# A running log-sum-exp on one core: the first-row test moves from small loads to GpSimd, and the last store is made whole

## The chip, the cores and the metric

The kernel runs on one NeuronCore of a Trainium2 chip. The core has five engines, each with its own in-order queue of instructions: TensorE (PE in the profile, PEld for its weight loads), VectorE (DVE), ScalarE (ACT), GpSimd (POOL) and SyncE (SP). They meet through semaphores. SBUF is the on-chip memory of 128 partitions, PSUM the memory that matmuls write. Transfers between HBM and SBUF run on 16 DMA engines that all the queues share; a transfer is cut into packets, and here each of the 16 engines gets the same number of them. The metric is the device time of one launch in microseconds (us). The kernel before takes 1264.43 us, the median of three runs from 1264.23 to 1265.02.

## The reference

The input `x` is float32 of shape (4, 4096, 4128): four batches, 4096 steps, 4128 columns. The output is the running log-sum-exp along the steps, for each batch and column by itself:

```python
out[:, 0, :] = x[:, 0, :].copy()
for t in range(1, S):
    mx = np.maximum(out[:, t - 1, :], x[:, t, :])
    out[:, t, :] = mx + np.log(np.exp(out[:, t - 1, :] - mx) + np.exp(x[:, t, :] - mx))
```

With values of moderate size this is log(cumsum(exp(x))). That is 270.5 MB read and 270.5 MB written.

## The kernel before

`_fast` computes log(cumsum(exp(x))) directly and also computes a flag that says whether that was safe. If it wasn't, `_general` computes everything again in the reference's slow form. With the inputs here the flag is good and `_general` is branched over, so it is code that lies in the program and doesn't run.

**Tiling.** A batch has 4096 rows. A step of the kernel (`Step`) takes 128 partitions times r rows, with r = 3: partition p holds rows 3p, 3p+1 and 3p+2 of the block, all 4128 columns, so a partition's share of a load is one run of 49,536 bytes. 4096 rows make ten steps of r = 3 and one of r = 2, eleven steps a batch and 44 in all. In the first batch the step of r = 2 comes first, in the others last. The first steps of the four batches are steps 0, 11, 22 and 33. A step's tile `xt` has four buffers. It is worked on in place, in four chunks of columns (`Chunk`): three of 1024 and a rest of 1056.

**Work of a step and chunk.** ScalarE takes Exp of the whole chunk (L114). VectorE adds the rows inside a partition (`sums`, L118: one instruction for r = 2, two for r = 3, each with two operands in SBUF). TensorE multiplies the last row by a triangle of ones (`excl`), which gives every partition the sum of the partitions before it (`head`, L125; for the rest `head_rest`, L133 and L135). VectorE adds this from PSUM to all rows (`add`, L149; `add_rest`, L142). TensorE passes the total of the last partition on to the next step (`pass_on`, L158), for the rest VectorE copies it (`keep`, L154). ScalarE takes Ln (L170). Then the whole tile is stored.

**Order.** The order on every engine is written out by hand in lists (`ORDER`, `DORDER`, `PORDER`) and recorded as such (`manual_schedule`). ScalarE's order in a step is: Exp of chunks 0 and 1, Ln of chunks 2 and 3 of the step before, Exp of chunks 2 and 3, Ln of chunks 0 and 1 (`e0 e1 p2 p3 e2 e3 l0 l1`). So store k can be issued only after the second pair of Ln in step k+1. VectorE's order is `s0 s1 a0 s2 a1 s3 a2 r` and then the carry copy. In the last step ScalarE ends with Ln of chunks 2 and 3.

**SP's queue** issues every transfer: four loads at the start, the loads of first rows (below), then store k, the load of step k+3 (which waits until store k-1 has landed and its buffer is free), store k+1, and so on. DMA engines take transfers in the order of issue.

**The flag.** At a batch's end VectorE sums the totals (`total`, L165) into columns of `part`. To see a too small first value as well, `load_first` (L198) loads the four first rows of `x` a second time, as four transfers of 16 KB onto 32 partitions (`first`), and `small` (L193) in step 22 takes exp(-x) of them with its sum into one more column of `part`. After the last step `part` is reduced, one matmul sums it over the partitions (L295), and the flag is whether the sum is at most 2^40 (L296). All five engines read the flag (L351) and branch (L352).

**The last store** (`SPLIT`) is cut in two by columns: columns 0 to 2047 are stored when Ln of chunks 0 and 1 is done, the rest when the other two are.

Of the kernel before, what the change touches and what calls it, by code (L numbers as in the profile page):

```python
# [7 lines left out]
FP32 = mybir.dt.float32  # L8
INT32 = mybir.dt.int32
ACT = mybir.ActivationFunctionType  # L10
AX = mybir.AxisListType
ALU = mybir.AluOpType
P = 128
R = 3
CH = 1024
# [4 lines left out]
LAST = ["e0", "e1", "p2", "p3", "e2", "e3", "l0", "l1", "l2", "l3"]  # L20
DORDER = ["s0", "s1", "a0", "s2", "a1", "s3", "a2", "r"]
PORDER = ["h0", "h1", "p0", "h2", "p1", "r0", "r1", "p2", "r2"]
SPLIT = True
HI = 96
LIMIT = float(2 ** 40)
STEPS = 15


def _constants(nc, pool):
# [22 lines left out]
def _fast(ctx, tc, x, out, flag):  # L52


    nc = tc.nc
    B, S, D = x.shape
# [8 lines left out]
    cpool = ctx.enter_context(tc.tile_pool(name="cpool", bufs=1))  # L65
# [1 line left out]
    prest = ctx.enter_context(tc.tile_pool(name="prest", bufs=2, space=bass.MemoryType.PSUM))  # L67

    carry = cpool.tile([P, rest], FP32, name="carry")
    q = 8  # L70
    first = cpool.tile([B * q, D // q], FP32, name="first")
    part = cpool.tile([P, 4 * B + 1], FP32, name="part")
    every = cpool.tile([P, 1], FP32, name="every")
    nc.vector.memset(carry, 0.0)  # L74
    nc.vector.memset(part, 0.0)
# [22 lines left out]
    class Chunk:  # L98
# [13 lines left out]
        def exp(self):  # L112
            rows = self.rows(0, self.t.r)
            nc.scalar.activation(rows, rows, ACT.Exp)  # L114

        def sums(self):
            for j in range(1, self.t.r):
                nc.vector.tensor_tensor(  # L118
                    out=self.row(j), in0=self.row(j - 1), in1=self.row(j), op=ALU.add)
# [48 lines left out]
        def ln(self):  # L168
            rows = self.rows(0, self.t.r)
            nc.scalar.activation(rows, rows, ACT.Ln)  # L170

    steps = []
    for b in range(B):
        n = S // P
# [3 lines left out]
        row = 0  # L178
# [4 lines left out]

    chunks = [Chunk(s, c) for s in steps for c in range(4)]
    T = len(steps)
    done = set()
    act, dve, pe, sync = [], [], [], []

    def put(queue, name, work, *needs):
        queue.append((name, work, needs))  # L190

    def small():
        nc.scalar.activation(  # L193
            first, first, ACT.Exp, scale=-1.0, accum_out=part[:first.shape[0], 4 * B:4 * B + 1])

    def load_first():
        for b in range(B):
            nc.sync.dma_start(  # L198
                out=first[b * q:(b + 1) * q, :], in_=x[b, 0, :].rearrange("(q f) -> q f", q=q))

    for k, t in enumerate(steps):
        C = chunks[4 * k:4 * k + 4]
        prev = chunks[4 * k - 4:4 * k] if k else []
        W = len(subs)

        def exp(c):
            put(act, ("exp", k, c), C[c].exp, ("load", k))

        def ln(kk, c):
            put(act, ("ln", kk, c), chunks[4 * kk + c].ln, ("keep" if c == 3 else "pass", kk, c))  # L210

        order = ORDER if 0 < k < T - 1 else (FIRST if k == 0 else LAST)
        for o in order:
            if o[0] == "e":
                exp(int(o[1]))
            elif o[0] == "l":
                ln(k, int(o[1]))
            elif k:
                ln(k - 1, int(o[1]))
        if k == T // 2:  # L220
            put(act, ("small",), small, ("first",))

        def sums(c):
            put(dve, ("sums", k, c), C[c].sums, ("exp", k, c))

        def add(c):
            put(dve, ("add", k, c), C[c].add, ("head", k, c))

        for o in DORDER:
            if o[0] == "s":  # L230
                sums(int(o[1]))
            elif o[0] == "a":
                add(int(o[1]))
            else:
                for i in range(W):
                    put(dve, ("rest", k, i), lambda i=i, C=C: C[3].add_rest(i), ("headr", k, i))
        put(dve, ("keep", k, 3), C[3].keep)
        if t.last and k < T - 1:
            for c in range(4):
                put(dve, ("total", k, c), C[c].total, ("keep" if c == 3 else "pass", k, c))  # L240

        def head(c):
            put(pe, ("head", k, c), C[c].head, ("sums", k, c), ("total", k - 1, c) if k and steps[k - 1].last else ("sums", k, c))

        def headr(i):
            put(pe, ("headr", k, i), lambda C=C: C[3].head_rest(i), ("sums", k, 3),
                ("keep", k - 1, 3) if k else ("sums", k, 3), ("rest", k, i - 2) if i >= 2 else ("sums", k, 3))

        def onward(c):
            put(pe, ("pass", k, c), C[c].pass_on, ("add", k, c))  # L250

        for o in PORDER:
            if o[0] == "h":
                head(int(o[1]))
            elif o[0] == "p":
                onward(int(o[1]))
            else:
                headr(int(o[1]))

        if k < BUFS:  # L260
            put(sync, ("load", k), t.load)
    put(sync, ("first",), load_first)
    for c in range(4):
        if any(o == f"p{c}" for o in LAST) and not any(o == f"l{c}" for o in LAST):
            put(act, ("ln", T - 1, c), chunks[-4 + c].ln, ("keep" if c == 3 else "pass", T - 1, c))
    for k, t in enumerate(steps):
        if k < T - 1:
            put(sync, ("store", k), t.store, *[("ln", k, c) for c in range(4)])
            if k + BUFS - 1 < T and k:
                put(sync, ("load", k + BUFS - 1), steps[k + BUFS - 1].load, ("store", k - 1))  # L270
        elif SPLIT:
            put(sync, ("half",), lambda: steps[-1].store(0, 2 * CH), ("ln", k, 0), ("ln", k, 1))
            put(sync, ("store", k), lambda: steps[-1].store(2 * CH), ("ln", k, 2), ("ln", k, 3))
        else:
            put(sync, ("store", k), t.store, *[("ln", k, c) for c in range(4)])
    queues = [sync, act, dve, pe]
    at = [0] * 4
    while any(at[i] < len(queues[i]) for i in range(4)):
        moved = False
        for i in range(4):  # L280
            while at[i] < len(queues[i]):
                name, work, needs = queues[i][at[i]]
                if not all(d in done for d in needs):
                    break
                work()
                done.add(name)
                at[i] += 1
                moved = True
        assert moved, [queues[i][at[i]][::2] for i in range(4) if at[i] < len(queues[i])]

    for c in chunks[-4:]:
        c.total()
# [1 line left out]
    q = prest.tile([P, MM], FP32, name="q")  # L294
# [4 lines left out]
def _general(ctx, tc, x, out):  # L299

    nc = tc.nc
    B, S, D = x.shape
    q = P // B
    f = D // q
    assert P == B * q and D == q * f and (S - 1) % STEPS == 0
    one = ctx.enter_context(tc.tile_pool(name="one", bufs=1))
    state = one.tile([P, f], FP32, name="state")
    xs = one.tile([P, STEPS, f], FP32, name="xs")
    os = one.tile([P, STEPS, f], FP32, name="os")
    mx = one.tile([P, f], FP32, name="mx")  # L310
    two = one.tile([P, 2, f], FP32, name="two")

    def flat(t, b, first, n):
        return t[b, bass.ds(first, n), :].rearrange("t (q f) -> q t f", q=q)

    for b in range(B):
        nc.gpsimd.dma_start(out=state[b * q:(b + 1) * q, :].unsqueeze(1), in_=flat(x, b, 0, 1))
    for b in range(B):
        nc.gpsimd.dma_start(out=flat(out, b, 0, 1), in_=state[b * q:(b + 1) * q, :].unsqueeze(1))
    with tc.For_i(1, S, STEPS) as i:  # L320
        for b in range(B):
            nc.gpsimd.dma_start(out=xs[b * q:(b + 1) * q], in_=flat(x, b, i, STEPS))
        for j in range(STEPS):
            own = state if j == 0 else os[:, j - 1, :]
            nc.vector.tensor_tensor(out=mx, in0=own, in1=xs[:, j, :], op=ALU.max)
            nc.vector.tensor_tensor(out=two[:, 0, :], in0=own, in1=mx, op=ALU.subtract)
            nc.vector.tensor_tensor(out=two[:, 1, :], in0=xs[:, j, :], in1=mx, op=ALU.subtract)
            nc.scalar.activation(two, two, ACT.Exp)
            nc.vector.tensor_tensor(
                out=two[:, 0, :], in0=two[:, 0, :], in1=two[:, 1, :], op=ALU.add)  # L330
            nc.scalar.activation(two[:, 0, :], two[:, 0, :], ACT.Ln)
            nc.vector.tensor_tensor(out=os[:, j, :], in0=mx, in1=two[:, 0, :], op=ALU.add)
        nc.vector.tensor_copy(state, os[:, STEPS - 1, :])
        for b in range(B):
            nc.gpsimd.dma_start(out=flat(out, b, i, STEPS), in_=os[b * q:(b + 1) * q])


@with_exitstack
# [46 lines left out]
```

## Time and profile before

| What | Value |
|---|---|
| Median of three runs | 1264.43 us (1264.23 to 1265.02) |
| The profiled execution | 1264.14 us, its span 1262.7 us |
| Bytes over the span | 541.47 MB, mean 429 GB/s |
| VectorE, ScalarE, TensorE, GpSimd busy | 82%, 73%, 60%, 0% |
| A load of r = 3 from issue to landing | 43.8 us (40 of them) |
| A store of r = 3 from issue to landing | 33.1 us (40 of them) |
| The loads of first rows | 4 of 16.1 KB |
| The two parts of the last store | 2048 and 2080 KB |
| Last Ln begins; its pair takes | 1243.76 us; 3.76 us |
| The flag's comparison (L296) | at 1250.38 us |

The profile shows one execution from its first to its last instruction (the span). The time of an execution is 1.4 us longer than its span. For each engine the profile has busy time, groups of instructions by line, and what ended the idle time in front of them. The chain of waits follows the work that ended last back to the start. The windows give each engine's busy time in a stretch, the share of time that the 16 DMA engines worked, and the rate at which they moved bytes. The timeline has the instructions of one engine in order: start, duration, line, operation, output and input; the SP queue's rows are the issues of transfers. The trace also holds every DMA packet and every landing, so one can see when each of the 16 engines ended its part of a transfer.

### The profile page before, as it was taken

The numbers are of one execution on the slowest core, as the hardware profiler recorded it, in microseconds if no ns is written. First come the engines' busy times: TensorE is split into PE (matmuls) and PEld (weight loads), VectorE is DVE, ScalarE is ACT, GpSimd is POOL, SyncE is SP. The second block draws the span as 40 slices with busy tenths as digits, with TensorE's granted clock in tenths as the row PEclk, the third lists the DMA queues.
The fourth block names the chain that finished last, engine by engine and source line by source line (L and its number), as shares of the span: only waits on it lengthen the run. The fifth ranks groups of instructions, "written<-read, shape, count | busy, mean of one in ns | idle before, by whom it ended". The sixth has DMA issues, their size and how long they took to land.

```text
span 1262.7 us, 4846 instructions
## 1 busy us (share of the span) xinstructions
PE 761.7 (60%) x1562; PEld 307.1 (24%) x1562; DVE 1031.7 (82%) x664; ACT 926.7 (73%) x355; POOL 1.1 (0%) x9
## 2 busy tenths in 40 slices
PE   4677755565665656665556666665665766665564
PEld 1222222222222222222222222222221222222221
DVE  4999977889878888888779888888878988887785
ACT  4987777777777767768578767667957867767793
POOL 0000000000000000000000000000000000000000
PEclk9898988888888888888788888888878888888887
DMA  9999999999999999999999999999999999999997
GB/s 410 412 429 439 430 428 434 436 429 427 438 432 435 429 435 435 432 432 429 435 434 435 432 430 435 436 430 430 433 438 428 440 432 430 435 436 427 433 424 328
DMA packets 13164, 541.47 MB, mean 429 GB/s; under 512 B 1456, under 2 KB 1456, under 8 KB 1488
## 3 DMA queue, kind: packets, MB, share of 16 engines
q1 hardware_dynamic: 13136, 541.14, 99.4%
q8 instruction: 13, 0.21, 0.1%
q14 instruction: 15, 0.12, 0.0%
HBM read 270.60 MB, written 270.53 MB: 429 GB/s over the span
## 4 chain that ended last, share of the span: by engine, by line
DMA 73%; ACT 11%; DVE 8%; issue 4%; PE 3%; ACTq 0%; SPq 0%
DMA xt<-in_x_dram 42%; DMA out_dram<-xt 31%; ACT xt L170 6%; ACT xt L114 5%; DVE xt L149 4%; DVE xt L118 3%; PE base L125 2%; DVE xt L142 1%; PE base L158 1%; DVE part L165 0%; DVE carry L154 0%; PE q L135 0%; PE q L133 0%; ACTq L170 0%; SPq L93 0%
## 5 line engine op out<-in xcount | busy, mean ns | idle before, releaser
L114 ACT ACTIVATE xt<-xt 128x3072 f32<-128x3072 f32 (+3 forms) x176 | 465.7, 2694 | 196.6 <-DMA xt<-in_x_dram 196.6
L125 PE MATMUL base<-xt,excl 128*128 128x512 f32 x528 | 342.9, 802 | 365.3 <-DVE xt L118 335.0
L170 ACT ACTIVATE xt<-xt 128x3072 f32<-128x3072 f32 (+3 forms) x176 | 470.4, 2696 | 123.2 <-PE base L158 122.8
L118 DVE TENSOR_TENSOR xt<-xt 128x1024 f32<-128x1024 f32 (+1 forms) x336 | 413.1, 1232 | 152.3 <-ACT xt L114 146.4
L149 DVE TENSOR_TENSOR xt<-xt,base 128x3072 f32<-128x3072 f32 (+1 forms) x132 | 429.4, 3253 | 57.2 <-PE base L125 57.2
L158 PE MATMUL base<-xt,pick 128*128 128x512 f32 x528 | 260.8, 616 | 115.5 <-DVE xt L149 115.5
L125 PEld LDWEIGHTS base<-xt,excl 128*128 128x128 f32 x528 | 129.9, 262 | 545.1 <-issue 509.4
L158 PEld LDWEIGHTS base<-xt,pick 128*128 128x128 f32 x528 | 90.1, 189 | 285.5 <-DVE xt L149 219.1
L142 DVE TENSOR_TENSOR xt<-xt,q 128x1536 f32<-128x1536 f32 (+1 forms) x132 | 153.6, 1215 | 5.9 <-PE q L135 5.9
L135 PE MATMUL q<-xt,excl 128*128 128x512 f32 (+1 forms) x264 | 106.2, 486 | 1.7 <-DVE xt L118 1.7
L133 PE MATMUL q<-carry,pick 128*128 128x512 f32 (+1 forms) x240 | 93.9, 473 | 0.0
L133 PEld LDWEIGHTS q<-carry,pick 128*128 128x128 f32 x240 | 44.5, 189 | 58.5 <-issue 30.1
L135 PEld LDWEIGHTS q<-xt,excl 128*128 128x128 f32 x264 | 45.6, 190 | 47.9 <-issue 46.4
L154 DVE COPY carry<-xt 32x1056 f32<-32x1056 f32 x44 | 31.1, 707 | 1.5
L165 DVE TENSOR_REDUCE part<-base 32x1 f32<-32x1024 f32 x12 | 14.1, 1223 | 0.1
L165 DVE TENSOR_REDUCE part<-carry 32x1 f32<-32x1056 f32 x4 | 4.9, 1236 | 0.0
L295 PE MATMUL q<-ones,every 128*1 128x1 f32 x2 | 0.2, 163 | 6.1 <-DVE every L293 6.1
L346 ACT ACT_TABLE_LOAD x1 | 1.3, 1283 | 1.0 <-PEq L369 1.0
L74 DVE MEMSET carry<- 128x1056 f32 x1 | 0.9, 938 | 1.3 <-PEq L369 1.3
L295 PEld LDWEIGHTS q<-ones,every 128*1 128x1 f32 x2 | 0.1, 80 | 6.1 <-issue 6.1
L193 ACT ACTIVATE first<-first 32x516 f32<-32x516 f32 x1 | 0.6, 616 | 0.0
L296 DVE TENSOR_SCALAR flag<-q 1x1 int32<-1x1 f32 x1 | 0.1, 147 | 0.4 <-PE q L295 0.4
(12 smaller groups left out, 1.9 us busy)
## 6 DMA issues: line engine op xcount, KB each, us to landing
xt<-in_x_dram SPq DMA_DIRECT2D x40, 6192.0 KB, 43.8
out_dram<-xt SPq DMA_DIRECT2D x40, 6192.0 KB, 33.1
xt<-in_x_dram SPq DMA_DIRECT2D x4, 4128.0 KB, 38.9
out_dram<-xt SPq DMA_DIRECT2D x3, 4128.0 KB, 29.4
out_dram<-xt SPq DMA_DIRECT2D x1, 2080.0 KB
out_dram<-xt SPq DMA_DIRECT2D x1, 2048.0 KB, 16.0
first<-in_x_dram SPq DMA_DIRECT2D x4, 16.1 KB
```

What stands on the lines that cost most here:

```text
L114: nc.scalar.activation(rows, rows, ACT.Exp)
L118: nc.vector.tensor_tensor(out=self.row(j), in0=self.row(j - 1), in1=self.row(j), op=ALU.add)
L125: nc.tensor.matmul(base[self.c][:, s:s + MM], lhsT=excl, rhs=own[:, s:s + MM], start=t.first, stop=True, skip_group_check=True)
L133: nc.tensor.matmul(q[:, :w], lhsT=pick, rhs=carry[:, s:s + w], start=True, stop=False, skip_group_check=True)
L135: nc.tensor.matmul(q[:, :w], lhsT=excl, rhs=self.row(t.r - 1)[:, s:s + w], start=t.first, stop=True, skip_group_check=True)
L142: nc.vector.tensor_tensor(out=rows, in0=rows, in1=self.q[i][:, :w].unsqueeze(1).to_broadcast([P, t.r, w]), op=ALU.add)
L149: nc.vector.tensor_tensor(out=rows, in0=rows, in1=base[self.c].unsqueeze(1).to_broadcast([P, t.r, CH]), op=ALU.add)
L154: nc.vector.tensor_copy(carry[HI:P, :], self.row(self.t.r - 1)[HI:P])
L158: nc.tensor.matmul(base[self.c][:, s:s + MM], lhsT=pick, rhs=self.row(self.t.r - 1)[:, s:s + MM], start=True, stop=False, skip_group_check ...
L165: nc.vector.tensor_reduce(out=part[HI:P, i:i + 1], in_=own[HI:P, :self.w], axis=AX.X, op=ALU.add)
L170: nc.scalar.activation(rows, rows, ACT.Ln)
L346: nc.scalar.preload_act_table_set("natural_log_exp_and_others")
```

## The change

The general path's transfers go from GpSimd's queue to SP's queue, and its loop takes one step of the sequence a turn instead of 15. The loads of first rows and the Exp of them are gone. In their place, in the first step of each batch, GpSimd reads row 0 of partition 0 of `xt` right after Exp of each chunk. For each column it writes 2^41 where the value is below 2^-40, and 0 elsewhere (`lowest`): the first chunk into `least`, every other one into `bad`, which is then added to `least`. The last chunk's 32 extra columns are a pass of their own. Each first step thus has four counts and three additions of 1024 columns and a count and an addition of 32, all on one partition. VectorE reduces `least` into a column of `part` four steps later (`lower`), behind the carry copy. VectorE's adds into a chunk wait for GpSimd's count of it, ScalarE's Ln of a first step's chunk waits for GpSimd's count and addition, a load into the buffer waits for GpSimd's last read of it, and GpSimd starts on a batch's first row only when `lower` of the batch before is done. The last store is one transfer. There are 88 transfers: 44 loads and 44 stores.

```diff
-SPLIT = True
+SPLIT = False
 HI = 96
 LIMIT = float(2 ** 40)
-STEPS = 15
...
-    q = 8
-    first = cpool.tile([B * q, D // q], FP32, name="first")
-    part = cpool.tile([P, 4 * B + 1], FP32, name="part")
+    least = cpool.tile([1, CH], FP32, name="least")
+    bad = cpool.tile([1, CH], FP32, name="bad")
+    part = cpool.tile([P, 5 * B], FP32, name="part")
...
+    heads = [k for k in range(T) if steps[k].first]
...
-    def small():
-        nc.scalar.activation(
-            first, first, ACT.Exp, scale=-1.0, accum_out=part[:first.shape[0], 4 * B:4 * B + 1])
-
-    def load_first():
-        for b in range(B):
-            nc.sync.dma_start(
-                out=first[b * q:(b + 1) * q, :], in_=x[b, 0, :].rearrange("(q f) -> q f", q=q))
+    def lowest(t, c):
+
+        for a in range(c * CH, (c + 1) * CH if c < 3 else D, CH):
+            w = min(CH, D - a)
+            row = t.xt[0:1, 0, a:a + w]
+            own = bad if a else least
+            nc.gpsimd.tensor_scalar(
+                out=own[:, :w], in0=row, scalar1=1.0 / LIMIT, scalar2=2 * LIMIT, op0=ALU.is_lt, op1=ALU.mult)
+            if a:
+                nc.gpsimd.tensor_tensor(out=least[:, :w], in0=least[:, :w], in1=bad[:, :w], op=ALU.add)
+
+    def lower(t):
+        i = 4 * B + t.b
+        nc.vector.tensor_reduce(out=part[0:1, i:i + 1], in_=least, axis=AX.X, op=ALU.add)
...
         def ln(kk, c):
-            put(act, ("ln", kk, c), chunks[4 * kk + c].ln, ("keep" if c == 3 else "pass", kk, c))
+            put(act, ("ln", kk, c), chunks[4 * kk + c].ln, ("keep" if c == 3 else "pass", kk, c),
+                *[("low", kk, c)] * steps[kk].first)
...
-        if k == T // 2:
-            put(act, ("small",), small, ("first",))
+        if t.first:
+            for c in range(4):
+                put(pool, ("low", k, c), lambda t=t, c=c: lowest(t, c), ("exp", k, c),
+                    *[("lower", j) for j in heads if j < k])
...
         put(dve, ("keep", k, 3), C[3].keep)
+        for j in heads:
+            if k == j + min(4, heads[1] - 1):
+                put(dve, ("lower", j), lambda j=j: lower(steps[j]), *[("low", j, c) for c in range(4)])
...
-    put(sync, ("first",), load_first)
...
-    for b in range(B):
-        nc.gpsimd.dma_start(out=state[b * q:(b + 1) * q, :].unsqueeze(1), in_=flat(x, b, 0, 1))
...
-    with tc.For_i(1, S, STEPS) as i:
-        for b in range(B):
-            nc.gpsimd.dma_start(out=xs[b * q:(b + 1) * q], in_=flat(x, b, i, STEPS))
-        for j in range(STEPS):
...
+    nc.sync.dma_start(out=state, in_=step(x, 0))
+    nc.sync.dma_start(out=step(out, 0), in_=state)
+    with tc.For_i(1, S, 1) as i:
+        nc.sync.dma_start(out=xs, in_=step(x, i))
...
+        nc.sync.dma_start(out=step(out, i), in_=state)
```

More of the change, by code (lines that the diff above doesn't have):

```diff
@@ L185, in _fast @@
     T = len(steps)
+    heads = [k for k in range(T) if steps[k].first]
     done = set()
-    act, dve, pe, sync = [], [], [], []
+    act, dve, pe, pool, sync = [], [], [], [], []
     def put(queue, name, work, *needs):
         queue.append((name, work, needs))
-    def small():
-        nc.scalar.activation(
-            first, first, ACT.Exp, scale=-1.0, accum_out=part[:first.shape[0], 4 * B:4 * B + 1])
-    def load_first():
-        for b in range(B):
-            nc.sync.dma_start(
-                out=first[b * q:(b + 1) * q, :], in_=x[b, 0, :].rearrange("(q f) -> q f", q=q))
+    def lowest(t, c):
[10 more added lines that the diff above has]
+        nc.vector.tensor_reduce(out=part[0:1, i:i + 1], in_=least, axis=AX.X, op=ALU.add)
     for k, t in enumerate(steps):
@@ L275, in _fast @@
             put(sync, ("store", k), t.store, *[("ln", k, c) for c in range(4)])
-    queues = [sync, act, dve, pe]
-    at = [0] * 4
-    while any(at[i] < len(queues[i]) for i in range(4)):
+    queues = [sync, act, dve, pe, pool]
+    at = [0] * 5
+    while any(at[i] < len(queues[i]) for i in range(5)):
         moved = False
-        for i in range(4):
+        for i in range(5):
             while at[i] < len(queues[i]):
@@ L288, in _fast @@
                 moved = True
-        assert moved, [queues[i][at[i]][::2] for i in range(4) if at[i] < len(queues[i])]
+        assert moved, [queues[i][at[i]][::2] for i in range(5) if at[i] < len(queues[i])]
     for c in chunks[-4:]:
@@ L304, in _general @@
     f = D // q
-    assert P == B * q and D == q * f and (S - 1) % STEPS == 0
+    assert P == B * q and D == q * f
     one = ctx.enter_context(tc.tile_pool(name="one", bufs=1))
     state = one.tile([P, f], FP32, name="state")
-    xs = one.tile([P, STEPS, f], FP32, name="xs")
-    os = one.tile([P, STEPS, f], FP32, name="os")
+    xs = one.tile([P, f], FP32, name="xs")
     mx = one.tile([P, f], FP32, name="mx")
     two = one.tile([P, 2, f], FP32, name="two")
-    def flat(t, b, first, n):
-        return t[b, bass.ds(first, n), :].rearrange("t (q f) -> q t f", q=q)
@@ L316, in _general @@
-    for b in range(B):
-        nc.gpsimd.dma_start(out=state[b * q:(b + 1) * q, :].unsqueeze(1), in_=flat(x, b, 0, 1))
-    for b in range(B):
-        nc.gpsimd.dma_start(out=flat(out, b, 0, 1), in_=state[b * q:(b + 1) * q, :].unsqueeze(1))
-    with tc.For_i(1, S, STEPS) as i:
-        for b in range(B):
-            nc.gpsimd.dma_start(out=xs[b * q:(b + 1) * q], in_=flat(x, b, i, STEPS))
-        for j in range(STEPS):
[L324 to L335, printed above, removed]
@@ new lines, in step @@
+    def step(t, i):
+        return t[:, bass.ds(i, 1), :].rearrange("b t (q f) -> b (t q) f", q=q)
+    nc.sync.dma_start(out=state, in_=step(x, 0))
+    nc.sync.dma_start(out=step(out, 0), in_=state)
+    with tc.For_i(1, S, 1) as i:
+        nc.sync.dma_start(out=xs, in_=step(x, i))
+        nc.vector.tensor_tensor(out=mx, in0=state, in1=xs, op=ALU.max)
+        nc.vector.tensor_tensor(out=two[:, 0, :], in0=state, in1=mx, op=ALU.subtract)
+        nc.vector.tensor_tensor(out=two[:, 1, :], in0=xs, in1=mx, op=ALU.subtract)
+        nc.scalar.activation(two, two, ACT.Exp)
+        nc.vector.tensor_tensor(
+            out=two[:, 0, :], in0=two[:, 0, :], in1=two[:, 1, :], op=ALU.add)
+        nc.scalar.activation(two[:, 0, :], two[:, 0, :], ACT.Ln)
+        nc.vector.tensor_tensor(out=state, in0=mx, in1=two[:, 0, :], op=ALU.add)
+        nc.sync.dma_start(out=step(out, i), in_=state)
```

## The prediction

> **What bounds the kernel now.** I read the shares, then the chain of waits, then the transfers, then the timeline of single queues. From the page:
>
> ```profile
> PE 761.7 (60%) x1562; PEld 307.1 (24%) x1562; DVE 1031.7 (82%) x664; ACT 926.7 (73%) x355; POOL 1.1 (0%) x9
> ...
> DMA  9999999999999999999999999999999999999997
> GB/s 410 412 429 439 430 428 434 436 429 427 438 432 435 429 435 435 432 432 429 435 434 435 432 430 435 436 430 430 433 438 428 440 432 430 435 436 427 433 424 328
> ...
> DMA 73%; ACT 11%; DVE 8%; issue 4%; PE 3%; ACTq 0%; SPq 0%
> ```
>
> VectorE is 82% busy, yet the chain is 73% DMA, and the 16 DMA engines are full in every slice but the last. The kernel is its bytes at one rate: the trace's packets of 49,536 B take 1.829 us each, 8 to a DMA engine per transfer, so 14.6 us a transfer. Compute can be late without cost while transfers are queued. So the question is where the queues run dry, or where the packets are slow. From the windows (columns: width, five engines, clock, DMA share, GB/s):
>
> ```profile
> 30.00:54.00 24.00, 17.76 (x35) 6.95 (x33) 22.18 (x15) 20.96 (x10) 0.00 (x0) 0.86 0.99 429
> 54.00:58.00 4.00, 2.35 (x8) 1.25 (x8) 3.97 (x5) 4.00 (x2) 0.00 (x0) 1.00 1.03 330
> ...
> 1256.00:1257.00 1.00, 0.00 (x0) 0.00 (x0) 0.00 (x0) 0.00 (x0) 0.00 (x0) 0.50 0.34 125
> 1257.00:1258.00 1.00, 0.00 (x0) 0.00 (x0) 0.00 (x0) 0.00 (x0) 0.00 (x0) 0.50 0.22 92
> 1258.00:1259.00 1.00, 0.00 (x0) 0.00 (x0) 0.00 (x0) 0.00 (x0) 0.00 (x0) 0.50 0.14 58
> ```
>
> Two places are weak. At 54 to 58 us, where the four loads of first rows pass, the rate falls to 330. After 1256 us only a few engines still work: a share of 0.14 is two of 16. The landings tell the same: the last store ends on most engines by 1255.9 us, on the two latest at 1260.8 and 1261.0. Those two fall behind by 0.3 to 1.4 us at a time through the run, mostly when instruction fetches share an engine. They never idle, so they set the end. The span ends 1.6 us after them.
>
> The timeline of SP's queue shows where a store comes closest to being late:
>
> ```profile
> 39.33 0.38 SPq L96 DMA_DIRECT2D out_dram<-xt  x1
> 63.99 0.37 SPq L96 DMA_DIRECT2D out_dram<-xt  x1
> 68.30 0.34 SPq L93 DMA_DIRECT2D xt<-in_x_dram  x1
> ...
> 1230.09 0.33 SPq L96 DMA_DIRECT2D out_dram<-xt  x1
> 1240.55 0.64 SPq L96 DMA_DIRECT2D out_dram<-xt  x1
> 1247.55 0.53 SPq L96 DMA_DIRECT2D out_dram<-xt  x1
> ```
>
> The load at 68.30 waits for store 0, whose packets end between 67.17 and 67.78 on the 16 engines. Store 1 is issued at 63.99 and can start 1.0 us later (the first load: issue 1.04, first packet 2.08). So it is there 2.2 to 2.8 us before the engines need it. That is the least margin of the run until the last steps; the stores around the later first steps have 5.8 us or more, and 12 us against the two late engines.
>
> **The change part by part.** The sum is made against the profiled execution: 1264.14 us, span 1262.7, 0.3 us below the median of 1264.43.
>
> (1) Four loads of first rows go. Their 32 packets of 2,064 B take 85 ns each, 0.17 us per DMA engine. But beside them the last packet of load 3 takes 2.5 to 3.2 us on all 16 engines in place of 1.83. From load 2's landing to store 0's it takes 25.4 to 25.5 us; one full transfer (14.63) and one short (9.78) make 24.4. So they cost 1.05 us, and everything after moves up by it: **-1.05**, with ends -0.17 (the stretch is not theirs) and -1.05. Their four issues (1.4 us of SP by 4.5 us) delay nothing, since SP's next work is at 39.33. The exp on them goes too (L193, 0.6 us), in step 22, where ScalarE waits some 5 us a step for its load: 0; without that wait, -0.6.
>
> (2) The last store is one transfer instead of two. Now each engine has 16 packets of 8,192 B at 0.309 and 16 of 8,320 B at 0.314: 10.0 us. The two late engines took 10.9, from 1250.13 to 1261.04, because the fetches after the final branch (four of 8 KB near 1255) share them. One transfer has 8 packets of 33,024 B at 1.222: 9.8 us. It is issued when the last Ln ends (1247.52), as the second half is now, and reaches the engines at 1248.6; the late two are free at 1250.13. So its lateness is hidden by their backlog, 1.5 us of cover. They gain 0.2 if the fetches hit them again and 1.1 if not: I take **-0.6**. The other 14 engines now wait and end at 1248.6 + 9.8 = 1258.4, still before the late two at 1259.9. With the cover gone (no late engines) 1258.4 would be the end, against 1255.9 for two halves: +2.5.
>
> (3) GpSimd counts the first row after Exp in steps 0, 11, 22 and 33: four counts and three additions of 1024 elements on one partition, and two of 32. GpSimd's rows:
>
> ```profile
> 0.64 0.10 POOL L369 MEMSET const-uint8-127<- 128x1 uint8 x1
> ...
> 1.18 0.20 POOL L42 MEMSET pick<- 128x128 f32 x1
> ...
> 1.66 0.29 POOL L43 TENSOR_SCALAR_AFFINE_SELECT pick<-pick 128x128 f32<-128x128 f32 x1
> ```
>
> 127 elements more cost 0.10 us in a memset and 0.19 in a select, so 1024 cost 0.9 or 1.7 us. The count reads, compares and writes as the select does: I take 1.7. The addition reads two tiles: between 1.7 and twice that, I take 2.4. Together 14.3 us in a step.
>
> Who waits: VectorE's adds of each chunk wait for its count, and ScalarE's Ln for count and add; behind them stand all later work of these in-order queues. Step 0, by its rows: the exps end at 15.4, 17.2, 19.0 and 20.9, so counts end at 17.1, 19.0, 23.1 and 27.2 and the last small addition near 29.9. The adds begin at 20.57, 23.91, 27.28, 29.48 and 32.00. Nothing waits; the nearest margin is 2.2 us. That is the low end, 0.
>
> The other end is that GpSimd's and VectorE's reads of SBUF take turns. No row of before has GpSimd beside VectorE. The instructions that read two SBUF operands are the sums (1.23 us):
>
> ```profile
> 22.77 1.22 DVE L118 TENSOR_TENSOR xt<-xt 128x1024 f32<-128x1024 f32 x1
> ...
> 26.11 1.25 DVE L118 TENSOR_TENSOR xt<-xt 128x1056 f32<-128x1056 f32 x1
> ...
> 33.03 2.49 DVE L118 TENSOR_TENSOR xt<-xt 128x1024 f32<-128x1024 f32 x2
> ```
>
> Turn by turn: sums 0 to 16.7, count 0 to 18.4, sums 1 to 19.6, count 1 to 21.3, addition to 23.7; sums 2 then begins at 23.7 in place of 22.77, sums 3 at about 29 in place of 26.11, and step 1's first sums near 35.7 in place of 33.03. From there to store 1 VectorE is on the chain, so store 1 is some 2.5 us late. Part (1) has eaten 1.05 of its margin of 2.2 to 2.8: 1.1 to 1.7 is left, and the DMA engines idle for 0.8 to 1.4 us, which nothing gives back. No row decides; a sum reads two streams from the memory that GpSimd then reads, so I take turns: **+1.1**, and keep 0. With 2.4 and 3.4 us for count and addition store 1 is 8 to 9 us late, +7: the far end.
>
> The Trainium skill bears on this twice, and both speak against the change. "SBUF — State Buffer", section "Who interferes with whom", says that a VectorE instruction with two SBUF inputs and a GpSimd instruction that reads SBUF exclude each other for a whole instruction; no run here shows it yet, and by it the sum has the +1.1, without it 0. "GPSIMD Engine Reference", section "Elementwise — side-by-side cycle accounting", gives 4497 ns for an addition of 2048 elements, so an estimate of 2.25 us for this one, which would make the term +1.0.
>
> In steps 11, 22 and 33 the same 2 to 3 us stay inside the 5.8 us of margin. A new load of the buffer also waits for GpSimd: 68.3 against some 30 to 35 us in step 0, hidden.
>
> (4) Four reductions of the counts on VectorE, 1.2 us each by L165's rows, stand after the carry copies of steps 4, 15, 26 and 37. VectorE waits there some 3 us for the next Exp, and the stores have 10 us: 0; uncovered, 1.2 each. They feed only the final sum, which ends at 1250.5 under the last store.
>
> (5) The general path is branched over; its rewrite moves no executed work, only code. A block of code more or less is a fetch of 0.31 us on one DMA engine: 0, with ends of 0.5 either way.
>
> Sum: -1.05 - 0.6 + 1.1 = -0.55, so 1263.6 for a profiled execution and **1263.9** on the median.
>
> **The rivals.** (A) No turns: GpSimd hides, and the sum is -1.65: 1262.8; with the whole -1.1 of part (2), 1262.3. For it: each count has 2 us of margin. To pass 1261.9 it needs the two late engines to fall behind less besides. (B) Slower: GpSimd's instructions are longer than I take them and step 0's stall reaches the DMA queues. It decides when store 1 is 5.3 us late or more, counts of 2.4 us and additions of 2.6 with turns. At 7 us late: 7 - 1.4 - 1.65 = +4, 1268.4. For it: the smallest margin of the run lies on this chain. Against: the select's row. (C) The stretch at 54 us belongs to the turn from loads to stores, not to the first rows: -0.17 - 0.6 + 0.3 (more margin is left to store 1) = -0.5, the same time. (D) The change does nothing that can be seen, the late engines covering all: also within the band.
>
> **How the numbers follow.** A measurement of this kernel can tell about 0.2%, 2.5 us, from no change: faster is below 1261.9, slower above 1267.0. Forecast with C and D 0.46, A 0.24, B 0.30. Of A half goes under 1261.9, since it ends only 0.4 to 0.9 us above it and the runs of before spread over 0.8 us: faster 0.12. Slower is B, 0.30. The rest, 0.58, is within. The range reaches to A's better half and through most of B: 1261.8 to 1268.6. The likeliest case alone spans 1262.3 to 1265.5.
>
> **What would show it.** GpSimd's counts near 1.7 us and additions near 2.4. Step 0's sums starting up to 3 us later behind them. Store 1 near 66.5 instead of 63.99; if it stays at 64, A. The rate in 54 to 58 us at 430. Load 4 issued near 67.3. A last transfer of some 10 us on the two late engines, and the span's end 1.6 us behind. I am wrong if GpSimd's instructions take 3 us, if VectorE is held in later first steps beyond 5.8 us, or if the last store starts after the late engines are free.

## The result and the profile after

The changed kernel takes 1270.46 us (median of six runs, 1269.74 to 1270.78), the kernel before 1264.33 beside it (1263.73 to 1265.02). The ratio is 1.0047, interval 1.0034 to 1.0060: **slower by 0.47%, 6.1 us**. The prediction was 1263.9 us with a range up to 1268.6, so the time lies above the range. The profiled execution took 1269.74 us, its span 1267.9.

The page of the changed kernel, the lines that answer to those of before:

```profile
PE 764.8 (60%) x1562; PEld 307.2 (24%) x1562; DVE 1046.8 (83%) x668; ACT 925.6 (73%) x353; POOL 101.2 (8%) x45
...
POOL 5200000000700000000070000000016000000000
...
DMA  9989999999999999999999999999999999999998
GB/s 408 415 358 409 432 436 432 431 433 430 432 439 426 436 436 427 437 433 434 427 434 436 436 425 438 437 427 437 433 434 432 429 436 434 429 436 433 430 426 349
...
DMA 66%; DVE 13%; ACT 11%; issue 4%; PE 3%; POOL 2%; ACTq 0%; SPq 0%; POOLq 0%; DVEq 0%
```

GpSimd works in four places, one for each batch. The rate differs from before in the third and fourth slices (63 to 127 us): 358 and 409 where 429 and 439 stood. POOL has entered the chain with 2% of the span, 24 us. That is one first step, not four. The rest of the run is the same in both: from store 2's landing on the slowest DMA engine to the last store's first packet there, 1137.3 us before (112.88 to 1250.13) and 1137.1 after (119.67 to 1256.80). So the loss is made before 120 us: from store 0's landing to store 2's it took 45.1 us and now takes 52.1.

SP's queue in the timeline of the changed kernel, in the stretch where before had 63.99 and 68.30:

```profile
71.39 0.34 SPq L95 DMA_DIRECT2D out_dram<-xt  x1
...
71.84 0.37 SPq L92 DMA_DIRECT2D xt<-in_x_dram  x1
```

Store 1 is issued 7.40 us later. The load behind it waited only for SP to get past store 1. The windows of the changed kernel (columns: width, busy time of PE, PEld, DVE, ACT and POOL, granted clock, DMA share, GB/s) show what that does:

```profile
54.00:58.00 4.00, 2.78 (x7) 1.06 (x6) 3.97 (x3) 1.11 (x2) 0.00 (x0) 1.00 1.01 330
58.00:67.00 9.00, 5.65 (x16) 2.36 (x14) 8.93 (x7) 9.00 (x4) 0.00 (x0) 1.00 0.95 411
67.00:72.00 5.00, 3.59 (x5) 1.55 (x6) 3.64 (x4) 5.00 (x3) 0.00 (x0) 0.51 0.00 0
```

Two things are to be read here. From 67 to 72 us nothing moves; before moved 476 GB/s in that stretch. Store 0 has landed on the 16 engines between 66.79 and 67.58, and store 1's first packets start between 72.24 and 72.39: the engines idle for 4.8 to 5.6 us, 5.2 in the mean. And at 54 to 58 us the rate is 330, the same as before, though no load of a first row is there any more.

What made store 1 late is GpSimd's timeline in step 0:

```profile
15.18 4.65 POOL L198 TENSOR_SCALAR least<-xt 1x1024 f32<-1x1024 f32 x1 [13.42 <-ACT xt L113]
19.81 3.62 POOL L198 TENSOR_SCALAR bad<-xt 1x1024 f32<-1x1024 f32 x1
23.51 2.37 POOL L201 TENSOR_TENSOR least<-least,bad 1x1024 f32<-1x1024 f32 x1
25.97 4.51 POOL L198 TENSOR_SCALAR bad<-xt 1x1024 f32<-1x1024 f32 x1
30.56 2.36 POOL L201 TENSOR_TENSOR least<-least,bad 1x1024 f32<-1x1024 f32 x1
33.01 3.62 POOL L198 TENSOR_SCALAR bad<-xt 1x1024 f32<-1x1024 f32 x1
...
39.15 0.31 POOL L198 TENSOR_SCALAR bad<-xt 1x32 f32<-1x32 f32 x1
```

Nothing here waits but the first: GpSimd works from 15.18 to 39.78 without a pause, 24.6 us where the prediction had 14.3. Counts of 1024 take 3.62 us or 4.5 to 4.65, not 1.7; additions take 2.36, near the 2.4 of the prediction. VectorE's timeline shows the wait (the brackets give the idle time before an instruction and who ended it):

```profile
15.13 1.23 DVE L117 TENSOR_TENSOR xt<-xt 128x1024 f32<-128x1024 f32 x1 [13.06 <-ACT xt L113]
16.93 1.40 DVE L117 TENSOR_TENSOR xt<-xt 128x1024 f32<-128x1024 f32 x1 [0.57 <-ACT xt L113]
19.91 2.29 DVE L148 TENSOR_TENSOR xt<-xt,base 128x2048 f32<-128x2048 f32 x1 [1.58 <-POOL least L198]
...
30.51 2.29 DVE L148 TENSOR_TENSOR xt<-xt,base 128x2048 f32<-128x2048 f32 x1 [3.51 <-POOL bad L198]
36.66 2.35 DVE L141 TENSOR_TENSOR xt<-xt,q 128x1024 f32<-128x1024 f32 x2 [3.86 <-POOL bad L198]
39.49 0.22 DVE L141 TENSOR_TENSOR xt<-xt,q 128x64 f32<-128x64 f32 x1 [0.48 <-POOL bad L198]
...
40.48 4.88 DVE L117 TENSOR_TENSOR xt<-xt 128x1024 f32<-128x1024 f32 x4
```

Step 1's sums, queued behind these adds, start at 40.48 in place of 33.03: 7.45 us late, which is store 1's lateness.

Yet 4.8 to 5.6 us of idle engines are not the whole of the 7.0 lost up to store 2's landing. The windows later on, again of the changed kernel:

```profile
84.00:88.00 4.00, 3.69 (x10) 1.43 (x9) 4.00 (x2) 4.00 (x2) 0.00 (x0) 1.00 1.08 384
88.00:98.00 10.00, 5.55 (x13) 2.51 (x12) 8.96 (x9) 10.00 (x5) 0.00 (x0) 0.83 0.93 402
98.00:102.00 4.00, 2.76 (x7) 0.87 (x5) 3.97 (x3) 4.00 (x2) 0.00 (x0) 1.00 1.26 400
```

Here transfers are queued and still the rate is 384 to 402. Store 1 ends and a load follows near 85 us, and a store follows that load near 100 us. Around these two changes of direction 21 and 23 packets are longer than others of their size, by 12.5 and 21.2 us in sum: over 16 engines 0.8 and 1.3 us. Nearly all of it lies in the last packets, one to an engine, of the transfer ahead of each change.

### The profile page after: what moved, and what is told of

Its sections match the earlier page's. It is cut to its first block, busy times and chain, and to the rows that moved or that the text cites. A ratio compares the mean times of both kernels' runs of the same rounds, so it can differ in the third digit from the quotient of the medians.

```text
span 1267.9 us, 4906 instructions
## 1 busy us (share of the span) xinstructions
PE 764.8 (60%) x1562; PEld 307.2 (24%) x1562; DVE 1046.8 (83%) x668; ACT 925.6 (73%) x353; POOL 101.2 (8%) x45
## 4 chain that ended last, share of the span: by engine, by line
DMA 66%; DVE 13%; ACT 11%; issue 4%; PE 3%; POOL 2%; ACTq 0%; SPq 0%; POOLq 0%; DVEq 0%
DMA xt<-in_x_dram 38%; DMA out_dram<-xt 29%; DVE xt L148 6%; ACT xt L169 6%; ACT xt L113 5%; DVE xt L117 4%; PE base L124 2%; DVE xt L141 2%; POOL bad L198 1%; DVE part L164 1%; POOL least L201 1%; PE base L157 0%; DVE carry L153 0%; POOL least L198 0%; PE q L134 0%
## 5 line engine op out<-in xcount | busy, mean ns | idle before, releaser
L117 DVE TENSOR_TENSOR xt<-xt 128x1024 f32<-128x1024 f32 (+1 forms) x336 | 423.2, 1263 | 134.9 <-ACT xt L113 129.0
L198 POOL TENSOR_SCALAR least<-xt 1x1024 f32<-1x1024 f32 x4 | 17.6, 4393 | 868.3 <-ACT xt L113 868.3
L198 POOL TENSOR_SCALAR bad<-xt 1x1024 f32<-1x1024 f32 (+1 forms) x16 | 53.4, 3339 | 1.2 <-ACT xt L113 0.2
L201 POOL TENSOR_TENSOR least<-least,bad 1x1024 f32<-1x1024 f32 (+1 forms) x16 | 29.2, 1824 | 1.3
L205 DVE TENSOR_REDUCE part<-least 1x1 f32<-1x1024 f32 x4 | 4.8, 1207 | 0.1
```

Of the source, the lines that this page charges most:

```text
L117: nc.vector.tensor_tensor(out=self.row(j), in0=self.row(j - 1), in1=self.row(j), op=ALU.add)
L198: nc.gpsimd.tensor_scalar(out=own[:, :w], in0=row, scalar1=1.0 / LIMIT, scalar2=2 * LIMIT, op0=ALU.is_lt, op1=ALU.mult)
L201: nc.gpsimd.tensor_tensor(out=least[:, :w], in0=least[:, :w], in1=bad[:, :w], op=ALU.add)
```

## The experiments

Three theories of the loss stood at the start, and the expectations name them by letters. **W**: the wait in step 0 is the whole loss, through store 1. **P**: GpSimd's reads of SBUF slow VectorE in all four first steps. **O**: the other parts of the change do it. After the first runs the question was what a late store 1 costs, and whether the parts costed at nothing were worth nothing. Two baselines are used: the kernel before, at 1264.15, 1264.32 and 1264.35 us in the three groups of runs, and the first kernel below, which the table calls e1.

**Counts everywhere but in step 0.**

```diff
+    tested = heads[1:]
...
-                *[("low", kk, c)] * steps[kk].first)
+                *[("low", kk, c)] * (kk in tested))
...
-        if t.first:
+        if k in tested:
...
-                    *[("lower", j) for j in heads if j < k])
+                    *[("lower", j) for j in tested if j < k])
...
-        for j in heads:
+        for j in tested:
```

> The changed kernel with GpSimd's counts in steps 11, 22 and 33 but not in step 0 (the first row of batch 0 is not tested). Theory W (wait): the loss is the wait of VectorE's adds in step 0 for GpSimd, which makes store 1 7.4 us late and leaves the DMA engines idle for 4.8 to 5.6 us and with slower packets for some 2 us more. Then all of it goes: about 1263.2 (1270.46 less 7.2), store 1 issued at 63.7 us, no idle DMA at 67 to 72 us. Rival P (port): GpSimd's reads lengthen VectorE's sums in all four first steps, a quarter of the loss each: about 1268.6. Rival O (other code: the general path, the whole last store): 1270.5.

Measured: 1262.88 us, ratio 0.9990 (0.9981 to 0.9999). The timeline of SP and the window of the stretch that was empty, in this kernel:

```profile
63.56 0.34 SPq L95 DMA_DIRECT2D out_dram<-xt  x1
```
```profile
67.00:72.00 5.00, 3.73 (x8) 1.35 (x8) 4.97 (x4) 4.13 (x2) 0.00 (x0) 1.00 0.94 406
```

Three first steps of GpSimd's work, with everything else of the change in place, cost nothing that can be measured. W holds, O falls.

**Counts in step 0 alone.** The same edit with `tested = heads[:1]`.

> The changed kernel with GpSimd's counts in step 0 alone (the first rows of batches 1 to 3 are not tested). Theory W: nothing is given back, 1270.5 within 0.5. Rival P: three quarters are given back, about 1265.5. Rival O: 1270.5, so against O only the run without step 0's counts decides.

Measured: 1270.34 us, 1.0050 (1.0036 to 1.0064), store 1 at 71.54, 5.1 to 5.75 us of idle engines. One step holds the whole loss, and P falls with it.

P's effect is there all the same, and is hidden. VectorE and GpSimd of the changed kernel in step 22:

```profile
633.62 5.59 DVE L117 TENSOR_TENSOR xt<-xt 128x1024 f32<-128x1024 f32 x4 [3.11 <-ACT xt L113]
...
644.04 4.15 DVE L117 TENSOR_TENSOR xt<-xt 128x1024 f32<-128x1024 f32 x2
...
651.38 3.87 DVE L117 TENSOR_TENSOR xt<-xt 128x1056 f32<-128x1056 f32 x2
```
```profile
633.68 4.65 POOL L198 TENSOR_SCALAR least<-xt 1x1024 f32<-1x1024 f32 x1 [292.18 <-ACT xt L113]
638.30 4.39 POOL L198 TENSOR_SCALAR bad<-xt 1x1024 f32<-1x1024 f32 x1
642.78 2.35 POOL L201 TENSOR_TENSOR least<-least,bad 1x1024 f32<-1x1024 f32 x1
645.22 4.48 POOL L198 TENSOR_SCALAR bad<-xt 1x1024 f32<-1x1024 f32 x1
649.78 2.34 POOL L201 TENSOR_TENSOR least<-least,bad 1x1024 f32<-1x1024 f32 x1
652.21 4.52 POOL L198 TENSOR_SCALAR bad<-xt 1x1024 f32<-1x1024 f32 x1
```

The sums take 5.59, 4.15 and 3.87 us here; elsewhere 4.88, 2.48 and 2.54. The stores around steps 11, 22 and 33 keep 6 us or more of margin, so none of it reaches the DMA engines.

**No additions.** Each chunk's count goes into columns of its own, as bf16, and nothing is added; the reduction reads all of them.

```diff
-    least = cpool.tile([1, CH], FP32, name="least")
-    bad = cpool.tile([1, CH], FP32, name="bad")
+    least = cpool.tile([1, D], mybir.dt.bfloat16, name="least")
...
-            own = bad if a else least
...
-                out=own[:, :w], in0=row, scalar1=1.0 / LIMIT, scalar2=2 * LIMIT, op0=ALU.is_lt, op1=ALU.mult)
-            if a:
-                nc.gpsimd.tensor_tensor(out=least[:, :w], in0=least[:, :w], in1=bad[:, :w], op=ALU.add)
+                out=least[:, a:a + w], in0=row, scalar1=1.0 / LIMIT, scalar2=2 * LIMIT, op0=ALU.is_lt, op1=ALU.mult)
```

> The changed kernel with each count written to its own columns of a bf16 tile, without GpSimd's additions; VectorE reduces 4128 columns instead of 1024. Theory W (GpSimd's wait in step 0 makes store 1 late): counts of 3.6 to 4.5 us end at 19.8, 23.5, 28 and 32 us, where VectorE would begin its work at 20.0, 23.5, 27.0 and 29.2; store 1 is some 2.5 to 3 us late against a margin of 2.2 to 2.9, so 0 to 0.8 us of idle DMA engines: 1262.9 to 1263.7, and up to 2 us more where the queues run dry and the packets after it are slow. Rival P (the reads beside VectorE cost, and the counts alone read the tiles): 1269 to 1270.5.

Measured: 1263.88 us, 0.9995 (0.9986 to 1.0004). GpSimd in step 0, the four counts and the count of 32 in one row:

```profile
15.13 15.72 POOL L196 TENSOR_SCALAR least<-xt 1x1024 bf16<-1x1024 f32 x5 [13.36 <-ACT xt L112]
```

It ends at 30.85, and VectorE waits for it once, 1.30 us. Store 1 is issued at 64.70, 0.7 us later than before and not the 2.5 to 3 us that were expected, with 1.1 to 1.8 us of margin left, and the DMA engines do not stop between store 0 and store 1. 8.9 us less of GpSimd's work in one step is worth 6.6 us.

**A count of one operation**, the comparison without the multiplication.

```diff
-                out=own[:, :w], in0=row, scalar1=1.0 / LIMIT, scalar2=2 * LIMIT, op0=ALU.is_lt, op1=ALU.mult)
+                out=own[:, :w], in0=row, scalar1=1.0 / LIMIT, scalar2=None, op0=ALU.is_lt)
```

> The changed kernel with counts of one operation (is less than) instead of two (is less than, times 2^41); a too small value then adds 1 and no longer fails the flag. It prices the count. If the second operation makes the 3.6 us, the count falls to the 1.7 us that the prediction took from the select's row, step 0's chain to 14 us, and the time to 1263 to 1264. If the count stays at 3.6 us, 1270.5. In between, W gives the time by the end of the last count: about 1 us for each us that store 1 is later than 66.3.

Measured: 1267.34 us, 1.0024 (1.0015 to 1.0034), store 1 at 68.53. From GpSimd's timeline of this kernel:

```profile
15.29 3.79 POOL L198 TENSOR_SCALAR least<-xt 1x1024 f32<-1x1024 f32 x1 [13.52 <-ACT xt L113]
19.06 2.76 POOL L198 TENSOR_SCALAR bad<-xt 1x1024 f32<-1x1024 f32 x1
...
24.32 3.62 POOL L198 TENSOR_SCALAR bad<-xt 1x1024 f32<-1x1024 f32 x1
```

The second operation costs 0.86 us a count (2.76 here against 3.62 in the changed kernel; the counts of 15.29 and 24.32 began beside a sum of VectorE and are longer for it). Store 1 comes 2.86 us earlier than in the changed kernel, and 3.1 us come back. The expectation, 1 us for each us after 66.3, allowed 2.2 us above e1; it is 4.5.

**Lateness without GpSimd.** No counts at all; in their place ScalarE does four, or eight, Exps of a tile of zeros (128x1024) ahead of the Ln that store 1 waits for. The lines show four; the other kernel has `range(8)`.

```diff
+    zero = cpool.tile([P, CH], FP32, name="zero")
+    waste = cpool.tile([P, CH], FP32, name="waste")
+    nc.vector.memset(zero, 0.0)
...
+    tested = []
...
+    def idle():
+        nc.scalar.activation(waste, zero, ACT.Exp)
...
+            if k == 2 and o == "p2":
+                for i in range(4):
+                    put(act, ("idle", i), idle)
```

> The changed kernel without any counts on GpSimd (no first row is tested), and with four Exp of 128x1024 into a scratch tile on ScalarE ahead of the two Ln that release store 1: 3.7 us. It asks whether lateness alone makes the loss. Theory W: store 1 is 3.7 us late, the DMA engines idle for 0.8 to 1.5 us: 1262.9 plus 1.2 is 1264.1, and up to 1266 if running dry has a price of its own. Rival (it is GpSimd's work and not the lateness): 1262.9.

> The same with eight, 7.4 us, as late as the changed kernel's store 1. Theory W: idle for 4.5 to 5.2 us and slower packets after it for some 2 us: 1269.5 to 1270.5. If running dry has no price of its own, 1267.9. Rival (GpSimd's work): 1262.9.

Measured: 1266.27 us, 1.0015 (1.0006 to 1.0024), and 1270.37 us, 1.0049 (1.0036 to 1.0063); the first lies a little above what was expected, the second within it. SP's timeline with four Exps, and with eight:

```profile
67.03 0.34 SPq L96 DMA_DIRECT2D out_dram<-xt  x1
```
```profile
71.09 0.34 SPq L96 DMA_DIRECT2D out_dram<-xt  x1
```

With eight Exps store 1 is as late as in the changed kernel, and the time is the same to 0.1 us, with no instruction on GpSimd. So lateness is the whole price. The kernels make a curve. Idle is the time for which the DMA engines stood between store 0 and store 1, from the trace's packets: its ends over the 16 engines (good to 0.15 us), and in brackets its mean. The price is the median above e1's (which had other runs of before beside it, so it is good to some 0.2 us). The last column is from the profiled execution alone: from store 0's end to store 2's, each as a mean over the 16 engines, less the mean idle time.

| Kernel | Store 1 issued | Idle, us | Median | Price | Store 0 to store 2 less idle |
|---|---|---|---|---|---|
| e1, no counts in step 0 | 63.56 | 0 | 1262.88 | 0 | 44.34 |
| No additions | 64.70 | 0 | 1263.88 | 1.0 | 44.35 |
| Four Exps | 67.03 | 0.45 to 1.2 (0.7) | 1266.27 | 3.4 | 46.07 |
| One operation | 68.53 | 1.8 to 2.8 (2.3) | 1267.34 | 4.5 | 46.10 |
| Eight Exps | 71.09 | 4.5 to 5.3 (5.0) | 1270.37 | 7.5 | 46.08 |
| The change | 71.39 | 4.8 to 5.6 (5.2) | 1270.46 | 7.6 | 46.17 |
| Counts in step 0 alone | 71.54 | 5.1 to 5.75 (5.3) | 1270.34 | 7.5 | 46.27 |

The runs of the kernel without additions spread from 1262.59 to 1265.18, so its 1.0 tells little. But an idle time of 0.45 to 1.2 us costs 3.4. There is a price of its own on running dry, and it doesn't grow with the idle time: the last column is 1.7 to 1.9 us above e1's in all five kernels that run dry. By the medians the price less the idle time is 2.1 to 2.7; that is rougher, since the idle time is that of one execution, and the rest of up to 1 us has no cause shown. The kernels that run dry all have longer packets at the next two changes of direction (12.2 and 19.7 us in sum with four Exps, 13.9 and 18.7 with eight); in the first two of the table they come to 2.3 to 2.5 and 3.0 to 3.1. The difference is the 1.7 to 1.9 us an engine. Why the packets are longer wasn't found.

**The last store, by itself and undone.** The kernel before with one last store, and the changed kernel with two (the lines below the other way round).

```diff
-SPLIT = True
+SPLIT = False
```

> The kernel before with the last store as one transfer. By the prediction's part (2) and the trace of after, where the two late DMA engines took 9.8 us for it instead of 10.9: 1.1 us faster than before if the fetches after the branch miss those two engines, 0.2 if not, so 1263.2 to 1264.1. Rival (the late engines don't cover it): 2.5 us slower, 1266.8.

> The changed kernel with its last store divided again, as in before. By the prediction's part (2) the whole store gains 0.6 us (0.2 to 1.1): 1271.1 here. If the form of the last store is worth nothing measurable: 1270.5. If the cover had failed in after (the late engines waiting for the last store), the division would bring up to 2.5 us: 1268.

Measured: 1263.97 us, 0.9998 (0.9989 to 1.0007), and 1270.67 us, 1.0052 (1.0038 to 1.0066). So the form of the last store is worth 0.2 us by both, below what can be told from nothing. On the two late engines the last bytes took 10.6 and 9.95 us; 10.9 in before (two stores) and 9.8 in the changed kernel (one). The end of the changed kernel in the windows:

```profile
1262.00:1264.00 2.00, 0.00 (x0) 0.00 (x0) 0.00 (x0) 0.00 (x0) 0.00 (x0) 0.50 1.14 483
1264.00:1266.00 2.00, 0.00 (x0) 0.00 (x0) 0.00 (x0) 0.00 (x0) 0.00 (x0) 0.50 0.21 87
1266.00:1267.00 1.00, 0.00 (x0) 0.00 (x0) 0.00 (x0) 0.00 (x0) 0.00 (x0) 0.50 0.00 0
```

The last packets start before 1266. Most engines end at 1265.1, the late two at 1266.6: 1.5 us apart, where before had 5. The cover of the prediction was there: the late two never waited for the last store.

**The general path by itself.** The kernel before with the rewritten `_general`.

```diff
...
-    with tc.For_i(1, S, STEPS) as i:
...
+    with tc.For_i(1, S, 1) as i:
...
```

> The kernel before with the general path of after, which isn't executed. Theory W: the same as before, 1264.3 within 0.4; the part of an execution outside its span is to be seen, which is 1.48 us before and 1.84 after. Rival O: some of the 6.1 us is here, 1265 to 1270.

Measured: 1263.42 us, 0.9993 (0.9984 to 1.0002). The first load is issued at 0.81 us instead of 1.04.

**Both of these parts, without the counts.**

> The kernel before with the two parts of the change that touch no step in between: the last store whole and the general path of after. First rows are still loaded. By the runs of each part alone (-0.2 and -0.7 us): 1263.4 against 1264.3. If the -0.7 was chance, 1264.1. If both parts have their sizes of the prediction's sum (-0.6 and 0): 1263.7. These lie within what a measurement tells, so the profile decides: the first load issued near 0.81 us instead of 1.04, the last store near 10.6 us on the late engines.

Measured: 1263.49 us, 0.9996 (0.9986 to 1.0005). The last bytes on the late engines took 9.8 us.

**No loads of first rows, nothing in their place.**

```diff
-            put(act, ("small",), small, ("first",))
...
-    put(sync, ("first",), load_first)
```

> The kernel before without its four loads of first rows and without the Exp on them: the first rows of the batches are not looked at. By the prediction's part (1) it gains 1.05 us: 1263.3, and load 2's landing to store 0's takes 24.4 us. If the stretch near 54 us belongs to the turn from loads to stores (rival C): 0 to -0.2, so 1264.1 to 1264.3, the same 25.4 to 25.5 us, and a rate near 330 GB/s there all the same.

Measured: 1264.10 us, 0.9998 (0.9989 to 1.0007). Its window:

```profile
54.00:58.00 4.00, 2.05 (x8) 0.95 (x6) 3.93 (x5) 4.00 (x3) 0.00 (x0) 1.00 0.99 330
```

The stretch stays, with no small transfer in it; load 2's landing to store 0's takes 25.1 to 25.3 us (25.4 to 25.5 before). So the small loads cost 0.2 to 0.3 us at most; the rest of the 1 us an engine belongs to the turn from loads to stores.

**A version of the change without its loss.** The first batch's row is tested as in before, by one load (on 16 partitions) and an Exp in step 22; GpSimd tests the other three.

```diff
+    q = 16
+    first = cpool.tile([q, D // q], FP32, name="first")
...
+    tested = heads[1:]
...
+        nc.sync.dma_start(out=first, in_=x[0, 0, :].rearrange("(q f) -> q f", q=q))
```

> The changed kernel with the first batch's row tested as in before (one load of 16 KB on 16 partitions after the first four loads, its Exp in step 22) and the other three by GpSimd in steps 11, 22 and 33, so that everything the kernel must test is tested. If GpSimd's work in step 0 is the whole loss and the load of a first row costs nothing: as without step 0's counts, 1262.9, store 1 issued near 63.6, no idle DMA engine there. If the small load takes its share of the prediction's -1.05: 1263.1. If something else of GpSimd's work costs: above 1264.3.

Measured: 1263.39 us (1263.15 to 1263.82), 0.9992 (0.9983 to 1.0001). Store 1 and the stretch that was empty:

```profile
63.66 0.34 SPq L97 DMA_DIRECT2D out_dram<-xt  x1
```
```profile
67.00:72.00 5.00, 3.92 (x8) 1.35 (x8) 4.97 (x4) 4.42 (x2) 0.00 (x0) 1.00 0.94 406
```

7.1 us faster than the change, and 1.0 below before, which is less than can be told from no difference.

## Why the prediction was wrong

**The step that failed is part (3), in the length of a count.** It was put at 1.7 us by the affine select's row, 0.19 us for 127 elements more. A count takes 3.62 us with VectorE idle; that GpSimd's instructions might take 3 us was one of the prediction's own signs of being wrong. Of the 1.9 us that were missing, the second operation of a count is 0.86; with one operation it still takes 2.76, and why that is more than the select's row gave, no run shows. The chain came to 24.6 us instead of 14.3, so VectorE's adds waited for the counts, which the prediction's times excluded, and store 1 was 7.4 us late instead of 2.5. The additions were right (2.36 against 2.4), by a value taken between two bounds of 1.7 and 3.4.

**The picture of taking turns was right for additions and in part for counts.** A count that starts beside a running sum takes longer by about what is left of the sum: the sum of 15.13 ends 1.18 us after the count of 15.18 began, and that count has 1.03 us more than 3.62; for the count of 25.97 it is 1.03 left and 0.89 more. A sum that starts beside a running addition waits in the same way. From VectorE's timeline in step 22, the first sums of two pairs:

```profile
644.04 2.17 DVE L117 TENSOR_TENSOR xt<-xt 128x1024 f32<-128x1024 f32 x1
...
651.38 1.87 DVE L117 TENSOR_TENSOR xt<-xt 128x1056 f32<-128x1056 f32 x1
```

The additions beside them had 1.09 and 0.74 us left, and the sums take 0.95 and 0.6 us more than the usual 1.22 and 1.27. The second sum of the pair of 644.04 starts just after the count of 645.22 had its turn and takes 1.94 us, 0.7 more. So a count that had to wait holds VectorE for some 0.7 us, and not for its whole length: the sum of 16.93 ran inside one in 1.40 us, where a turn would have held it until 19.83. The prediction drew on the rule of the Trainium skill, "SBUF — State Buffer", section "Who interferes with whom", that such instructions exclude each other; these rows agree with it where VectorE came first and where an addition did, and for a whole count of GpSimd's they do not. In step 0 the turns made 1.9 us of 24.6; without them store 1 would still be some 5.5 us late (an estimate, 7.4 less 1.9), so they were not what decided.

**A term was missing.** The prediction let store 1's lateness beyond the margin be the loss, one for one. The runs show 1.7 to 1.9 us more up to store 2, 2.1 to 2.7 by the medians, as soon as the engines stop at all. Rival B has the same gap: its formula at 7.4 us gives 7.4 - 1.4 - 1.65 = 4.4 where 6.1 was measured.

**Part (1) credited 1.05 us that isn't there.** Rival C was right: the first rows' loads cost 0.2 to 0.3 us at most, within what rival C gave them (0.17) and the noise, and so hardly any of store 1's margin was eaten. **Part (2)**, -0.6 with ends of -0.2 and -1.1, came out at its small end, 0.2 by the times, which can't be told from nothing. Its cover held. **Part (4)** and the later first steps were hidden, as said. **Part (5)** was put at 0 within 0.5 either way; measured 0.7 to 0.9 less time, alone and together with the whole store, each with an interval that includes none. 0.23 us of it is the earlier start; the rest is not shown to be more than noise.

With the measured terms the sum closes. Kernel before with both small parts, 1263.5; the engines' mean idle time, 5.2; the slower packets up to store 2, 1.8: 1270.5, as measured (with 2.4, the price by the medians, 1271.1).

**The chances.** Slower had 0.30, through rival B, whose mechanism and place are what happened. Part (3)'s far end (store 1 8 to 9 us late, +7) had the size too, but the range stopped at 1268.6: it was drawn just past B's case of 7 us and not to the end of the one cost that no row bounded well.

## What to carry to other kernels

Find the transfer with the smallest margin first, and follow what is added on an engine to that transfer alone: the same work cost 7.5 us in step 0 and nothing in three later steps. Where no row shows an operation on an engine, take a row for its start-up only and let the range reach to the far end of its price, since the chance of a wait depends on it. And count DMA queues that run dry as a switch: in this kernel an idle time of 1.2 us at most cost 3.4.

## What had not been expected of the hardware

- DMA engines that all stopped once, for 0.5 to 5.6 us, had longer packets at the next two changes between stores and loads, 32 to 36 us in sum over 16 engines, whatever the length of the stop (five kernels). The first change of the run, near 54 us, has the same in every kernel (14 to 18 us in sum), with and without small transfers beside it. What makes the packets longer is not shown.
- GpSimd took 2.76 us for one comparison over 1024 elements of one partition, 3.62 us with a multiplication in the same instruction, 2.36 us for an addition of two tiles. One input was dearer than two.
- A sum of VectorE that started under an addition of GpSimd was held nearly to the addition's end (2.17 us against 1.22 with 1.09 us left), while one inside a count of 4.65 us took 1.40. A count that started under a sum took 0.8 to 1.0 us more.
